# A two-layer hybrid decoder: smaller first FFN group, GpSimd products in pieces, and four reorderings at the seams

## The chip, the cores and the metric

The kernel runs on one core of a Trainium2 chip. The metric is device time in microseconds (us) of one execution; the times below are of whole executions, and the trace is of one more execution under the hardware profiler. The core has TensorE (PE), which multiplies matrices and transposes, VectorE (DVE), ScalarE (ACT) and GpSimd (POOL), and SyncE (SP), whose queue issues all transfers.

## The reference

A token stream `x` of 1024 tokens by 1024 features goes through two layers and a last norm. All of it is float32.

```python
for i in range(DEPTH):                       # 2
    proj = rms_norm(h, attn_norm[i]) @ w_in[i]
    # six latent (MLA) heads, five sparse (DSA) heads with a top-256 of an indexer's
    # scores, five stick-breaking heads, for blocks of 128 queries
    mix = heads(proj)
    h = h + mix @ w_o[i]
    hf = rms_norm(h, ffn_norm[i])
    h = h + (silu(hf @ w_gate[i]) * (hf @ w_up[i])) @ w_down[i]     # 2816 wide
    g = sigmoid(rms_norm(h, ple_norm[i]) @ w_ple_gate[i])
    h = h + g * (p[i] @ w_ple_proj[i])
return rms_norm(h, final_norm)
```

A stick-breaking head weighs key j of query t by sigmoid(z_j) times the product of sigmoid(-z) over the keys between j and t.

## The kernel before, in words

Activations lie with features on the 128 partitions and 512 tokens (a "half") in the free dimension; there are two halves and eight feature tiles of the stream, `h[0]` to `h[7]`. Every product in float32 is done as three matmuls on rounded parts (lines 266, 267, 268): weight and activation are each split into a high part and the rest, and high x high, high x rest and rest x high are summed in one PSUM tile. Of the weights (`load_cols`), ScalarE makes the high part `wh` (line 187) and GpSimd the rest `wl`, in pieces of 256 columns (line 196). Of the activations, ScalarE makes the high part and VectorE the rest.

Work is woven from two streams. The dense stream (`first`, then `layer_rest` for each layer and half) runs the output projection `w_o`, the FFN, the gated embedding (PLE) and the next layer's input projection. The attention stream (`attention`) of the next half in order runs between its matmuls. The order on TensorE is the program's own order; on the other engines and in SyncE's queue a planner with a model of times sets it when the kernel is built. Under the last half's dense part (`layer_rest(1, 1)`) no attention is left to run.

- **FFN.** 22 feature tiles (`FT`), taken in groups of four: 4, 4, 4, 4, 4, 2. For each tile, a gate and an up projection (48 matmuls) and a chain of VectorE, ScalarE and GpSimd operations (lines 624 to 641; GpSimd's is line 627) make the tile's two parts. The down projection of a group (`down`) runs behind the first tile of the next group; the last group's runs on its own behind the last tile. It goes over eight output tiles m, and for each adds its PSUM tile to `h[m]` (line 590); the last one also hands `h[m]` to the next norm (`Norm.tile`): the scaled parts (lines 314, 315), a square (325), and a sum of squares `acc` (326). PSUM has three such D tiles.
- **Norm.** `rstd` turns `acc` into row sums by TensorE (line 344) and then works out the inverse root in 12 small VectorE operations (347 to 355). `after(n, f)` runs `f` n steps later; a step is three matmuls of a dense product.
- **Stick-breaking.** For two blocks of queries at a time, ScalarE makes `P` and `A` of up to 1024 keys, VectorE runs a scan over `A` (905), GpSimd multiplies `P` by it in one instruction (908), and TensorE transposes `P` in 128 x 128 pieces (845), 256 keys at a time: `piece(0)` needs columns 0 to 255 of both.
- **The start** of `layer_rest(1, 1)` loads eight tiles of `mix` (549): four into the attention's tiles `PT`, four into the three `tmp` tiles which the dense stream also uses. ScalarE and VectorE split them (292, 293).
- **The output.** For half 0 the row sums and eight `piece`s (four transposes, a scaling and a store each) follow as hooks in the next dense part. For half 1 they end the kernel: row sums, then eight pieces one after the other, each reading all four `h` of its column.
- **The beginning.** `load_x(0)` queues half of x, the norm gains, the first weights, the other half of x. `to_features` transposes x (1206).

Of the kernel before, what the change touches and what calls it, by code (L numbers as in the profile page):

```python
# [88 lines left out]
def trunk(ctx: ExitStack, tc, x, p, w_in, attn_norm, mla_q_norm, mla_w_uq, mla_kv_norm, mla_w_ukv,  # L89
# [35 lines left out]
    def spare_tile(m):  # L125

        if m < 6:
            return ap.tile([128, T], F32, name="P" if m < 4 else "A", bufs=4 if m < 4 else 2)[:, :HALF]
        if m == 6:
            return ap.tile([128, T], F32, name="kraw")[:, :HALF]  # L130
        return ap.tile([128, NT, 64], F32, name="vraw").rearrange("p t c -> p (t c)")
# [45 lines left out]

    def split_w(raw, hi, lo, *order):
# [32 lines left out]
    def load_x(half):  # L211
        xt = []
        for c in range(2):
# [6 lines left out]
            if half == 0 and c == 0:  # L220
                load_gains()
                first_w.append(load_cols([w_in[0, :, a:b] for a, b in FIRST], DT))
# [75 lines left out]
    class Norm:  # L298
# [8 lines left out]
        def tile(self, src):  # L307
# [14 lines left out]
            else:  # L322
                with priority(AHEAD if late else 0):
                    sq = tmp_tile()
                    ACT.activation(sq, src, AF.Square)
                    (DVE if late or alone[0] else POOL).tensor_tensor(self.acc, self.acc, sq, op=ALU.add)  # L326
# [208 lines left out]
    def layer_rest(L, half):  # L535
        k = (L, half)
        mix = {}
        final = L == DEPTH - 1 and half == 1
        for i, j in enumerate(MIX_ORDER):
            if i >= 4:  # L540
                a = tmp_tile()
# [16 lines left out]
        def add(m, ps):  # L558
            hm = spare_tile(m) if final else h_tile()
# [48 lines left out]
        for g0 in range(0, FT, FG):  # L608
            fs = range(g0, min(g0 + FG, FT))
            act = []  # L610
            if fs[-1] == FT - 1:
                pr = wp.tile([128, 4, PLE], F32, name="wr", bufs=WR)
                nc.sync.dma_start(pr, p[L, 0, half * HALF:(half + 1) * HALF].rearrange("(t p) c -> p t c", p=128))
            for f in fs:
                if f == FT - 1:
                    for j in range(2):
                        after(2 + 8 * j, lambda j=j: embedding(pr, j))
# [4 lines left out]
                def gate(pg=pg, G=G, t=t):  # L622
                    with priority(EVAC):
# [3 lines left out]
                        POOL.tensor_tensor(t, t, ffn.rep, op=ALU.mult)  # L627
# [72 lines left out]
        def piece(t, c, tile):  # L700
            ps = tile()
            for d in range(4):
                PE.transpose(ps[:, d * 128:(d + 1) * 128], h[c * 4 + d][:, t * 128:(t + 1) * 128], identF)  # L703
            o = act_tile(F32)
            if c:
# [4 lines left out]
            nc.sync.dma_start(out[0, tt * 128:(tt + 1) * 128, c * HALF:(c + 1) * HALF], o)  # L710

        if half == 0:
            after(4, norm.rstd)
            for i in range(8):
                after(12 + 2 * i, lambda i=i: piece(i % 4, i // 4, T_tile))
            return
        norm.rstd()
# [600 lines left out]
```

## Time and profile before

| | |
|---|---|
| time, median of three runs (lowest, highest) | 3173.28 us (3171.9, 3175.07) |
| profiled execution, its time | 3165.42 us |
| profiled execution, its span | 3163.4 us |
| mean granted clock of TensorE over the span | 0.988 |
| busy share of the span: DVE, ACT, POOL | 67%, 47%, 54% |

The time of an execution holds a little more than the span from the first to the last instruction; here 2.0 us. The profiled execution is 7.9 us below the median of the runs.

### The profile page before, as it was taken

The page shows a single profiled execution, that of the slowest core. Times are in us where ns is not written, and L with a number is a line of the kernel's source. Part 1 is how long each engine was busy: PE and PEld are TensorE (multiplying, and loading weights), DVE is VectorE, ACT ScalarE, POOL GpSimd, SP SyncE. Part 2 cuts the span into 40 slices and gives each one's busy share as a digit, 9 for nine tenths or more (in the row PEclk, how much of TensorE's full clock was granted, in tenths as well). Part 3 has the DMA queues.
Part 4 walks back from the last instruction along what each step waited for, and adds up shares of the span by engine and source line. Part 5 has one row for each costly group of instructions (what it writes and reads, how often), then busy time and mean ns, then how long its engine had stood idle before and what let it go on. Part 6 is the DMA issues. An engine that isn't in the chain of part 4 may idle for free. (4 is left out here: it accounts for less than half of the span.)

```text
span 3163.4 us, 43510 instructions
## 1 busy us (share of the span) xinstructions
PE 3053.9 (97%) x15059; PEld 2552.8 (81%) x15059; DVE 2107.8 (67%) x3716; ACT 1484.1 (47%) x2485; POOL 1722.8 (54%) x1965
## 2 busy tenths in 40 slices
PE   8999999999999999999999999989999999999998
PEld 6777878777887888888888888777888887888876
DVE  4879756799997645687744636899996565322234
ACT  4555654445455545444444535545444455322233
POOL 4543366666445433776555744666445445666663
PEclk9999999999999999999999999999999999999998
DMA  7475553333333446433332466323323223333332
GB/s 205 119 200 143 158 166 91 96 90 88 97 103 96 108 116 178 138 104 109 109 107 85 122 162 183 114 66 102 97 90 111 83 75 124 109 97 97 99 95 67
DMA packets 549948, 363.59 MB, mean 115 GB/s; under 512 B 134671, under 2 KB 491743, under 8 KB 549727
## 3 DMA queue, kind: packets, MB, share of 16 engines
q1 hardware_dynamic: 549727, 360.81, 39.3%
q8 instruction: 119, 1.95, 0.3%
q14 instruction: 102, 0.84, 0.1%
HBM read 310.65 MB, written 50.08 MB: 114 GB/s over the span
## 5 line engine op out<-in xcount | busy, mean ns | idle before, releaser
L196 POOL TENSOR_TENSOR wl<-wr,wh 128x256 fp32r<-128x256 f32 x1684 | 1395.6, 860 | 1147.5 <-ACT wh L187 1111.5
L266 PE MATMUL D<-act,wh 128*128 128x512 f32 x3416 | 1361.0, 398 | 10.5 <-ACT act L640 2.5
L267 PE MATMUL D<-act,wh 128*128 128x512 f32 x3416 | 1342.3, 393 | 5.7 <-DVE act L315 3.4
L268 PE MATMUL D<-act,wl 128*128 128x512 f32 x3416 | 1342.0, 393 | 3.5 <-POOL wl L196 3.3
L268 PEld LDWEIGHTS D<-act,wl 128*128 128x128 f32 x3416 | 645.4, 189 | 148.0 <-POOL wl L196 6.6
L187 ACT CAST wh<-wr 128x1024 fp32r<-128x1024 f32 (+3 forms) x432 | 443.7, 1027 | 678.9 <-PE D L267 551.5
L266 PEld LDWEIGHTS D<-act,wh 128*128 128x128 f32 x3416 | 647.3, 189 | 137.8 <-ACT act L640 3.5
L267 PEld LDWEIGHTS D<-act,wh 128*128 128x128 f32 x3416 | 646.7, 189 | 134.2 <-DVE act L315 5.1
L1099 DVE TENSOR_SCALAR_CACHE_REDUCE junk<-isc,cand 128x512 uint8<-128x512 f32 (+5 forms) x396 | 371.6, 938 | 5.8
L853 DVE TENSOR_TENSOR PT<-T,PT 128x384 fp32r<-128x384 f32 (+1 forms) x320 | 201.8, 631 | 94.9 <-ACT PT L852 94.2
L852 ACT CAST PT<-T 128x384 fp32r<-128x384 f32 (+1 forms) x320 | 173.4, 542 | 120.4 <-PE T L845 115.8
L862 PEld LDWEIGHTS O<-PT,V 128*128 128x128 f32 x1280 | 195.4, 190 | 33.4 <-DVE mix L871 9.3
L805 PE MATMUL S<-kh,qh 128*128 128x384 f32 (+4 forms) x544 | 206.7, 381 | 10.8 <-ACT P L891 5.6
L845 PE MATMUL T<-identF,P 128*128 128x128 f32 x1152 | 182.5, 275 | 32.8 <-POOL P L908 30.9
L862 PE MATMUL O<-PT,V 128*128 128x256 f32 x1280 | 205.9, 284 | 6.0 <-DVE mix L871 6.0
L805 PE MATMUL S<-kl,qh 128*128 128x384 f32 (+4 forms) x544 | 203.5, 375 | 2.5 <-DVE kl L293 2.5
L908 POOL TENSOR_TENSOR P<-P,A 128x127 f32<-128x127 f32 (+3 forms) x80 | 103.2, 1294 | 163.8 <-DVE A L905 103.3
L845 PEld LDWEIGHTS T<-identF,P 128*128 128x128 f32 x1152 | 135.0, 141 | 37.6 <-POOL P L908 34.5
L1065 DVE SCALAR_TENSOR_TENSOR isc<-P,iw,isc 128x384 f32<-128x384 f32 (+2 forms) x84 | 96.0, 1143 | 85.4 <-ACT P L1059 85.1
L627 POOL TENSOR_TENSOR tmp<-tmp,rr 128x512 f32<-128x512 f32 x88 | 119.6, 1359 | 39.4 <-DVE tmp L626 35.6
L891 ACT ACTIVATE P<-S,nm 128x128 f32<-128x128 f32 (+3 forms) x116 | 79.6, 687 | 125.1 <-DVE nm L884 124.6
L624 DVE TENSOR_TENSOR tmp<-D,rr 128x512 f32<-128x512 f32 x88 | 60.5, 688 | 102.1 <-PE D L268 97.6
(213 smaller groups left out, 3263.1 us busy)
## 6 DMA issues: line engine op xcount, KB each, us to landing
wr<-in_w_gate_dram SPq DMA_DIRECT2D x88, 512.0 KB, 3.8
wr<-in_w_up_dram SPq DMA_DIRECT2D x88, 512.0 KB, 3.9
wr<-in_w_down_dram SPq DMA_DIRECT2D x80, 512.0 KB, 3.4
wr<-in_w_in_dram SPq DMA_DIRECT2D x44, 512.0 KB, 3.9
wr<-in_w_in_dram SPq DMA_DIRECT2D x76, 256.0 KB, 3.5
wr<-in_w_o_dram SPq DMA_DIRECT2D x32, 512.0 KB, 4.0
wr<-in_w_ple_gate_dram SPq DMA_DIRECT2D x32, 512.0 KB, 3.7
h<-h SPq DMA_DIRECT2D x56, 256.0 KB, 4.4
```

The source lines that it names most:

```text
L187: ACT.copy(hi, raw)
L196: POOL.tensor_tensor(l[:, ks], a[:, ks], f32(h[:, ks]), op=ALU.subtract)
L266: PE.matmul(ps, a, ah, start=first and i == 0, stop=False)
L267: PE.matmul(ps, a, al, start=False, stop=False)
L268: PE.matmul(ps, b, ah, start=False, stop=last and i == len(ks) - 1)
L627: POOL.tensor_tensor(t, t, ffn.rep, op=ALU.mult)
L805: PE.matmul(o, a, b, start=j == 0, stop=j == len(mms) - 1)
L845: PE.transpose(ps[:, o:o + 128], self.P[q][:, j * 128:(j + 1) * 128], identF)
L852: ACT.copy(pt[:, 0, o:], self.ps[:, o:])
L853: DVE.tensor_sub(pt[:, 1, o:], self.ps[:, o:], f32(pt[:, 0, o:]))
L862: PE.matmul(self.O[:, :256], self.head.V[:, j, :], pt[:, s, o:o + 256], start=j == 0 and s == 0, stop=j == 2 * self.n - 1 and s == 1)
L1099: DVE.tensor_scalar(junk[:, :n], isc[:, off[t]:off[t] + n], c[:, i:i + 1], None, op0=op, op1=ALU.add, accum_out=cnt[:, i:i + 1])
```

## The change

The FFN's first group has two feature tiles and the others four: 2, 4, 4, 4, 4, 4; the load of `p` stays at feature tile 20. In the last dense part all eight spare tiles are taken at once, and the last four `mix` loads go into the second halves of attention's four `P` tiles. In `load_x(0)` all of x is queued ahead of the first weights. GpSimd's products of lines 326, 627 and 908 are issued in pieces of 256 columns. For half 0, the hook of the row sums moves from 4 to 10 steps, and the eight pieces from 12.. to 18... For half 1, 25 of the 32 transposes of the output stand ahead of the row sums, seven behind them, and then come the eight scalings, in turn on VectorE and ScalarE.

```diff
--- before.py
+++ after.py
@@ -122,13 +122,12 @@
     def h_tile():
         return dp.tile([128, HALF], F32, name="h", bufs=8)
 
-    def spare_tile(m):
-
-        if m < 6:
-            return ap.tile([128, T], F32, name="P" if m < 4 else "A", bufs=4 if m < 4 else 2)[:, :HALF]
-        if m == 6:
-            return ap.tile([128, T], F32, name="kraw")[:, :HALF]
-        return ap.tile([128, NT, 64], F32, name="vraw").rearrange("p t c -> p (t c)")
+    def spare_tiles():
+
+        P = [ap.tile([128, T], F32, name="P", bufs=4) for _ in range(4)]
+        A = [ap.tile([128, T], F32, name="A", bufs=AS) for _ in range(2)]
+        return ([t[:, :HALF] for t in P + A] + [ap.tile([128, T], F32, name="kraw")[:, :HALF],
+                 ap.tile([128, NT, 64], F32, name="vraw").rearrange("p t c -> p (t c)")], [t[:, HALF:] for t in P])
 
     def tmp_tile(dt=F32):
         return dp.tile([128, HALF], dt, name="tmp", bufs=TMPS)
@@ -175,6 +174,13 @@
 
 
 
+    def in_pieces(out, a, b, op):
+
+        n = out.shape[1]
+        for i in range(0, n, PIECE):
+            c = slice(i, min(i + PIECE, n))
+            POOL.tensor_tensor(out[:, c], a[:, c], b[:, c], op=op)
+
     def split_w(raw, hi, lo, *order):
 
         if order:
@@ -219,7 +225,8 @@
                 xt[c].append(a)
             if half == 0 and c == 0:
                 load_gains()
-                first_w.append(load_cols([w_in[0, :, a:b] for a, b in FIRST], DT))
+        if half == 0:
+            first_w.append(load_cols([w_in[0, :, a:b] for a, b in FIRST], DT))
         return xt
 
     gains = {}
@@ -323,7 +330,10 @@
                 with priority(AHEAD if late else 0):
                     sq = tmp_tile()
                     ACT.activation(sq, src, AF.Square)
-                    (DVE if late or alone[0] else POOL).tensor_tensor(self.acc, self.acc, sq, op=ALU.add)
+                    if late or alone[0]:
+                        DVE.tensor_tensor(self.acc, self.acc, sq, op=ALU.add)
+                    else:
+                        in_pieces(self.acc, self.acc, sq, ALU.add)
 
         def tokens(self, xt):
 
@@ -536,9 +546,11 @@
         k = (L, half)
         mix = {}
         final = L == DEPTH - 1 and half == 1
+        if final:
+            spare, more = spare_tiles()
         for i, j in enumerate(MIX_ORDER):
             if i >= 4:
-                a = tmp_tile()
+                a = more[i - 4] if final else tmp_tile()
             elif final:
                 if i % 2 == 0:
                     pair = ap.tile([128, 2, HALF], F32, name="PT", bufs=PTS)
@@ -556,7 +568,7 @@
             return load_cols([w_o[L, :, m * 128:(m + 1) * 128]], DT)
 
         def add(m, ps):
-            hm = spare_tile(m) if final else h_tile()
+            hm = spare[m] if final else h_tile()
             nc.sync.dma_start(hm, h_d[half][m])
             with priority(EVAC):
                 DVE.tensor_add(hm, hm, ps)
@@ -605,13 +617,13 @@
                 yield from gemm(ps, w, act, range(len(fs)), m0=(m % 2) * 128)
                 add(m, ps)
 
-        for g0 in range(0, FT, FG):
-            fs = range(g0, min(g0 + FG, FT))
+        for end in range(FT % FG or FG, FT + 1, FG):
+            fs = range(max(end - FG, 0), end)
             act = []
-            if fs[-1] == FT - 1:
-                pr = wp.tile([128, 4, PLE], F32, name="wr", bufs=WR)
-                nc.sync.dma_start(pr, p[L, 0, half * HALF:(half + 1) * HALF].rearrange("(t p) c -> p t c", p=128))
             for f in fs:
+                if f == FT - 2:
+                    pr = wp.tile([128, 4, PLE], F32, name="wr", bufs=WR)
+                    nc.sync.dma_start(pr, p[L, 0, half * HALF:(half + 1) * HALF].rearrange("(t p) c -> p t c", p=128))
                 if f == FT - 1:
                     for j in range(2):
                         after(2 + 8 * j, lambda j=j: embedding(pr, j))
@@ -624,7 +636,7 @@
                         DVE.tensor_mul(G, pg, ffn.rep)
                         ACT.activation(t, G, AF.Tanh, scale=0.5)
                         DVE.scalar_tensor_tensor(t, t, 1.0, G, op0=ALU.add, op1=ALU.mult)
-                        POOL.tensor_tensor(t, t, ffn.rep, op=ALU.mult)
+                        in_pieces(t, t, ffn.rep, ALU.mult)
                 pu = D_tile()
                 wu = load_cols([w_up[L, :, f * 128:(f + 1) * 128]], DT)
                 if f == 0:
@@ -697,28 +709,42 @@
             yield from in_projection(L + 1, half, norm, h)
             return
 
-        def piece(t, c, tile):
-            ps = tile()
-            for d in range(4):
-                PE.transpose(ps[:, d * 128:(d + 1) * 128], h[c * 4 + d][:, t * 128:(t + 1) * 128], identF)
-            o = act_tile(F32)
-            if c:
+        def turned(ps, i, ds):
+
+            for d in ds:
+                PE.transpose(ps[:, d * 128:(d + 1) * 128], h[i // 4 * 4 + d][:, i % 4 * 128:(i % 4 + 1) * 128], identF)
+
+        def put(ps, i):
+            o, t = act_tile(F32), i % 4
+            if i >= 4:
                 ACT.activation(o, ps, AF.Copy, scale=norm.r[:, t:t + 1])
             else:
                 DVE.tensor_scalar(o, ps, norm.r[:, t:t + 1], None, op0=ALU.mult)
             tt = half * 4 + t
-            nc.sync.dma_start(out[0, tt * 128:(tt + 1) * 128, c * HALF:(c + 1) * HALF], o)
+            nc.sync.dma_start(out[0, tt * 128:(tt + 1) * 128, i // 4 * HALF:(i // 4 + 1) * HALF], o)
+
+        def piece(i):
+            ps = T_tile()
+            turned(ps, i, range(4))
+            put(ps, i)
 
         if half == 0:
-            after(4, norm.rstd)
+            after(10, norm.rstd)
             for i in range(8):
-                after(12 + 2 * i, lambda i=i: piece(i % 4, i // 4, T_tile))
+                after(18 + 2 * i, lambda i=i: piece(i))
             return
+
+        S = S_tile()
+        banks = [S[:, 0], S[:, 1], psO.tile([128, HALF], F32, name="O"), T_tile(), D_tile(), D_tile(), D_tile()]
+        for i in range(7):
+            turned(banks[i], i, range(4 if i < 4 else 3))
         norm.rstd()
-        S = S_tile()
-        tiles = [S[:, 0], S[:, 1], T_tile(), T_tile(), psO.tile([128, HALF], F32, name="O"), D_tile(), D_tile(), D_tile()]
-        for i in range(8):
-            piece(i % 4, i // 4, lambda: tiles[i])
+        for i in range(4, 7):
+            turned(banks[i], i, (3,))
+        banks.append(T_tile())
+        turned(banks[7], 7, range(4))
+        for i in (0, 4, 1, 5, 2, 6, 3, 7):
+            put(banks[i], i)
 
 
     def attention(L, half):
@@ -905,7 +931,7 @@
                 DVE.tensor_tensor_scan(A[:, :n][:, ::-1], A[:, :n][:, ::-1],
                                        zeros[:, 0:1].to_broadcast([128, n]),
                                        initial=1.0, op0=ALU.mult, op1=ALU.add)
-                POOL.tensor_tensor(P[:, :n - 1], P[:, :n - 1], A[:, 1:n], op=ALU.mult)
+                in_pieces(P[:, :n - 1], P[:, :n - 1], A[:, 1:n], ALU.mult)
                 self.P.append(P)
 
         mixes, rows = {}, {}
```

## Rows read from the trace of the kernel before

**Rows 1.** The page of the profile, its first part: busy time, share of the span and instructions of each engine.

```profile
PE 3053.9 (97%) x15059; PEld 2552.8 (81%) x15059; DVE 2107.8 (67%) x3716; ACT 1484.1 (47%) x2485; POOL 1722.8 (54%) x1965
```

**Rows 2.** The view of waits of TensorE (PE) over the whole span: the waiting line and whom it waited for, then us in total, how often, the longest in us.

```profile
PE T L845 <- POOL P L908: 30.9, 12, 3.9
PE T L344 <- DVE rr L326: 9.6, 6, 3.1
...
PE D L1206 <- DMA act<-in_x_dram: 7.0, 6, 3.5
...
PE D L267 <- DVE act L315: 3.4, 3, 1.5
```

**Rows 3.** The view of windows: for each stretch of the span its length, the busy time and instructions of each engine, the granted clock of TensorE (1.00 is 2.4 GHz, 0.50 is 1.2 GHz) and the DMA share. Four stretches that each follow a wait of TensorE.

```profile
632.80:636.20 3.40, 3.40 (x10) 2.66 (x9) 3.36 (x7) 0.81 (x1) 2.51 (x4) 0.50 0.63 187
...
2216.50:2220.00 3.50, 3.24 (x9) 2.68 (x10) 3.50 (x7) 1.10 (x2) 3.50 (x6) 0.51 0.17 58
2670.50:2677.30 6.80, 5.97 (x13) 4.42 (x14) 3.55 (x11) 2.47 (x4) 0.00 (x0) 0.50 0.34 119
3090.40:3097.20 6.80, 6.80 (x21) 5.32 (x20) 3.48 (x15) 0.00 (x0) 0.00 (x0) 0.50 0.21 63
```

**Rows 4.** The view of lines by form for GpSimd (POOL), whole span: line, engine, operation, tiles and shapes, count | busy us, mean ns of one | idle us before them and who ended it.

```profile
L196 POOL TENSOR_TENSOR wl<-wr,wh 128x256 fp32r<-128x256 f32 x1668 | 1384.3, 861 | 1138.4 <-ACT wh L187 1102.4 <-PE T L845 15.1 <-DMA qraw<-dq 5.4
...
L908 POOL TENSOR_TENSOR P<-P,A 128x1023 f32<-128x1023 f32 x10 | 21.6, 2158 | 16.3 <-DVE A L905 5.9 <-DVE inc L1113 5.8 <-PE D L268 4.6
...
L908 POOL TENSOR_TENSOR P<-P,A 128x767 f32<-128x767 f32 x10 | 15.4, 1544 | 14.0 <-DVE A L905 9.0 <-DVE rstd L355 2.7 <-DVE cand L1114 2.4
...
L908 POOL TENSOR_TENSOR P<-P,A 128x127 f32<-128x127 f32 x10 | 4.1, 412 | 13.4 <-DVE inc L1113 6.2 <-DVE A L905 4.4 <-DVE rstd L355 2.4
```

**Rows 5.** The timeline (start us, length us, engine, line, operation, tiles and shapes, count [idle before it <- releaser]) of GpSimd, VectorE (DVE) and TensorE at three places: a stick-breaking product at 629 us, a weight split at 1757 us, another at 2087 us.

```profile
629.39 2.00 POOL L908 TENSOR_TENSOR P<-P,A 128x1023 f32<-128x1023 f32 x1
629.41 2.00 DVE L1113 TENSOR_SCALAR inc<-cnt 128x4 int32<-128x4 f32 x1
631.45 0.55 PE L845 MATMUL T<-identF,P 128*128 128x128 f32 x3 [3.69 <-POOL P L908]
637.33 0.60 PE L845 MATMUL T<-identF,P 128*128 128x128 f32 x4
...
1757.11 4.16 POOL L196 TENSOR_TENSOR wl<-wr,wh 128x256 fp32r<-128x256 f32 x4
1758.34 0.50 PE L268 MATMUL D<-act,wl 128*128 128x512 f32 x1 [0.81 <-POOL wl L196]
...
2087.47 5.83 POOL L196 TENSOR_TENSOR wl<-wr,wh 128x256 fp32r<-128x256 f32 x4 [1.62 <-ACT wh L187]
```

**Rows 6.** The timeline of TensorE at the start of the last down projection of layer 0, half 0.

```profile
969.44 0.40 PE L267 MATMUL D<-act,wh 128*128 128x512 f32 x1
969.68 0.40 PE L268 MATMUL D<-act,wl 128*128 128x512 f32 x1
972.53 0.50 PE L266 MATMUL D<-act,wh 128*128 128x512 f32 x1 [2.46 <-ACT act L640]
974.22 0.79 PE L267 MATMUL D<-act,wh 128*128 128x512 f32 x1 [1.18 <-DVE act L641]
974.81 0.63 PE L268 MATMUL D<-act,wl 128*128 128x512 f32 x1
975.23 0.63 PE L266 MATMUL D<-act,wh 128*128 128x512 f32 x1
```

**Rows 7.** The timeline of SyncE's queue (SPq) and TensorE at the start of the last output projection.

```profile
2666.59 1.00 SPq L549 DMA_DIRECT2D tmp<-mix  x2
...
2667.91 1.02 PE L344 MATMUL T<-ones,rr 128*128 128x1 f32 x8 [2.11 <-DVE rr L326]
2671.33 0.80 PE L266 MATMUL D<-act,wh 128*128 128x512 f32 x1 [2.39 <-ACT act L292]
```

**Rows 8.** The timeline of SyncE's queue, ScalarE (ACT) and TensorE at the start of the kernel.

```profile
6.74 2.00 SPq L218 DMA_DIRECT2D act<-in_x_dram  x4
...
11.36 1.04 ACT L187 CAST wh<-wr 128x1024 fp32r<-128x1024 f32 x1 [0.40 <-DMA wr<-in_w_in_dram]
...
12.09 1.05 PE L1206 MATMUL D<-identF,act 128*128 128x128 f32 x2 [1.76 <-DMA act<-in_x_dram]
...
13.47 3.64 PE L1206 MATMUL D<-identF,act 128*128 128x128 f32 x14 [0.33 <-DMA act<-in_x_dram]
...
16.77 0.78 PE L266 MATMUL D<-act,wh 128*128 128x512 f32 x1
```

**Rows 9.** The timeline of all engines at the end of the kernel.

```profile
3148.18 1.66 PE L344 MATMUL T<-ones,rr 128*128 128x1 f32 x8 [3.06 <-DVE rr L326]
...
3152.33 0.75 DVE L708 TENSOR_SCALAR act<-S,rstd 128x512 f32<-128x512 f32 x1
3153.11 7.07 SPq L710 DMA_DIRECT2D out_dram<-act  x8
3153.13 1.12 PE L703 MATMUL S<-identF,P 128*128 128x128 f32 x4 [2.34 <-DVE act L708]
...
3158.55 1.27 ACT L706 ACTIVATE act<-D,rstd 128x512 f32<-128x512 f32 x2 [0.17 <-PE D L703]
...
3158.68 0.27 PE L703 MATMUL D<-identF,kraw 128*128 128x128 f32 x1
```

## The prediction

> **What bounds the kernel now.** I read the engines' shares first: TensorE is busy for 97% of the span [rows 1], so only two things can shorten it, less work on TensorE or fewer of its waits. The change removes no matmul. I therefore went to the waits of TensorE [rows 2], then to the timeline around each, then to the granted clock behind it. The reader should see three things. The largest wait is not for weights but for the stick-breaking product on GpSimd: 30.9 us in 12 waits. The next ones belong to seams: row sums that wait for a norm's sum of squares (9.6 us), the first transposes that wait for x (7.0 us), a projection that waits for a norm's scaled parts (3.4 us). And a wait is paid twice: behind many of those of 2 us and more stands a stretch at the lower clock [rows 3], in which matmuls start 0.42 us apart (974.81 to 975.23) where they stood 0.24 us apart before it (969.44 to 969.68) [rows 6]. At those spacings a stretch at 1.2 GHz loses 43% of its length: 1.5 us of one of 3.4 us, 2.9 us of one of 6.8 us.
>
> **GpSimd's products in pieces.** Of the waiting product, TensorE needs columns 0 to 255 first. In rows 5 the product of 1023 columns runs from 629.39 for 2.00 us, and three transposes start at 631.45 after a wait of 3.69 us. That a reader may start on the first piece is shown at 1757: GpSimd works on four weight pieces from 1757.11 for 4.16 us, and the matmul that needs the first starts at 1758.34 [rows 5]. One piece costs, on the line through 127 columns (412 ns) and 767 (1544 ns), 1.77 ns per column and 0.64 us for 256; the weight pieces of that size take 0.86 us on average [rows 4]. Waiting products have 767 or 1023 columns, so a wait shrinks by 1544 - 861 = 0.68 us at least and 2158 - 640 = 1.52 us at most: 8 to 18 us over 12 waits. I take 14, nearer the upper end, since the one in rows 5 is a 1023. Below that the bound is nothing, should the earlier links (a late scan, weights ahead in GpSimd's queue) move by as much; above it the whole 30.9 us. Shorter waits also leave fewer stretches at the lower clock. Behind these waits I count six, the first at 632.8 and the last at 2216.5 [rows 3], one of them (2093.7) 6.8 us long, the others 3.4: 5 x 1.5 + 2.9 = 10.4 us lost, of which I take 6. Sum: -20 us (bounds 0 and -41).
> The extra cost, four pieces for 4 x 0.64 = 2.56 us where one took 2.00, falls on later columns; their transposes come at 637.33, 5.9 us behind the first [rows 5], which hides it. The pieces of lines 326 and 627 lengthen work that hides under a projection of 24 matmuls, 24 x 0.24 = 5.8 us; I cost them at nothing, and at 0.4 us for each of the 88 gate chains if the cover fails.
> There is a second effect. A VectorE operation on 128 x 4 elements (line 1113) starts at 629.41 and lasts 2.00 us, as long as the GpSimd product beside it [rows 5]: something holds it until the product ends. With pieces it would be held 0.64 us. I book nothing for it. The Trainium skill (SBUF - State Buffer, Who interferes with whom) says why: the two share a pair of ports, taken for a whole instruction, and the second to issue blocks fully. By that rule the change also gives VectorE gaps in which to step in, which is the rival below.
>
> **Groups of 2, 4, 4..** No matmul is added; what changes is the cover of the last down projection. With two tiles, 2 x 3 matmuls stand ahead of the first use of the last tile's parts; these came late by 2.46 us (high part, 972.53) and again by 1.18 us (rest, 974.22), and then ran at the lower clock [rows 6]. With four, 6 x 3 matmuls (4.3 us) stand there, 2.9 us more. And the norm's work per output tile gets 12 matmuls (2.9 us) instead of six (1.4 us). At these four seams: 3.6 us [rows 6] + 1.5 us for its stretch at 1.2 GHz + the 3.4 us for scaled parts (line 315) [rows 2] + 2.9 us for the stretch at 3090.4 [rows 3] + about 2 us of the row sums' 9.6: of these, 2.1 us stand at the last mix [rows 7] and 3.1 at the end [rows 9], and of the remaining 4.4 I take half. Sum -13.4 us; I take -13 (bounds -5 and -18). Against it, the group of two now stands first, woven with attention: its evacuations come every 1.4 us while VectorE also serves the heads. I add +4 us (0 to +9). The load of `p` stays where it was and costs nothing.
>
> **The last mix.** Two waits stand here: 2.11 us for the sum of squares (the moved hook gives it 6 x 3 matmuls, 4.3 us, more) and 2.39 us for a split whose load was queued only at 2666.59, when a `tmp` tile came free [rows 7]. Behind them 6.8 us run at 1.2 GHz [rows 3]. All gone: 2.1 + 2.4 + 2.9 = 7.4 us. Splits that come earlier press on VectorE, so I take -6.5 (bounds -2 and -8: if only the hook helps, the split is still late). The eight pieces move with the hook under later `w_o` matmuls; their stores pass in SyncE's queue among weight loads and cost nothing there, as the queue has two further weight buffers to run ahead.
>
> **The end.** Before, TensorE sits idle 3.06 us ahead of the row sums; second transposes wait 2.34 us for the first scaling; scalings go on from 3152.33 to 3158.55 + 1.27 = 3159.8, because transposes run between them [rows 9]. After, 25 transposes fill the idle time: four took 0.60 us [rows 5], so 2.8 us from 3145.1, or 3.8 at the worst, against row sums at 3148.2. Then eight scalings of 0.75 and 0.64 us run two at a time, 3.1 us instead of 7.5. That would give 4.4 us; but eight stores of 256 KB, issued over 7.07 us before [rows 9], have to land in a shorter time, so I take -2.5 (bounds 0 and -5).
> The Trainium skill (TensorE: Matmul & The Clock Gate, PE-mode transpose) says that transposes do not engage the full clock; by that rule the 25 would be done late, row sums would start some 2 us later, and the end would give nothing. Here four took 1.12 us at 3153.13, and with nothing but transposes in between one took 0.27 us at 3158.68 [rows 9], as at 637.33, where four took 0.60 us [rows 5]: the full clock came, which speaks against the rule.
>
> **The beginning.** The second half of x is queued at 6.74 us, behind the weights; transposes wait 1.76 us for it and end near 17.1, and the first product starts at 16.77. Weights arrive for ScalarE at 11.36 [rows 8]. After, x comes earlier by the two weight loads and the weights later by four x loads; the product could start when both are there, at about 14.5. I take -2 us (bounds +1.5 and -2.5).
>
> **Sum.** -20 - 13 + 4 - 6.5 - 2.5 - 2 = -40 us. Against the profiled execution's 3165.4 us this is 3125.4; the runs' median lies 7.9 us above it, so 3133.3, predicted 3133 us, 1.3% less. A change of 0.2% (6.3 us) is about what can be told from none.
>
> **The rivals.**
> - *Likeliest, 0.60:* as summed, 3133 us, own range 3120 to 3148.
> - *The pieces bring nothing, 0.20.* The wait's start is a scan on a full VectorE or weights ahead of the product, and the planner puts other pieces in front. For it: in the stretch at 2087 four weight pieces take 5.83 us [rows 5] just before a product. Against: even then the first piece still ends earlier than the whole. Time: 3133 + 20 = 3153 us.
> - *VectorE steps between the pieces, slower, 0.05.* Place: the products of 640 and more columns, 40 of them. If four pieces stretch as the weight pieces at 2087 did, to 5.83 us, the last ones end about when the next transposes come, 5.9 us on [rows 5]. The other parts give 20 us, so this ends slower by more than 0.2% once each of the 40 costs TensorE (20 + 6.3) / 40 = 0.66 us. At 1 us: 3173.3 + 40 - 20 = 3193 us. Against it: only the columns from 256 on are concerned, and each step needs 256 more.
> - *The new order costs elsewhere, 0.08.* The planner reorders four engines for the new program; other waits grow by as much as the seams give. 3133 + 36 = 3169, about no change.
> - *More than forecast, 0.07.* Nearly all of the product waits and their slow stretches go, and VectorE, no longer held, is ahead: 3133 - 21 = 3112 us.
>
> **How the numbers follow.** Faster: the first and last case, nearly all of the second, a quarter of the fourth, 0.88; same: half of the fourth and the edge of the second, 0.05; slower: the third and the last quarter of the fourth, 0.07. The range holds 8 in 10 if it leaves out the third and part of the fourth and last: 3112 to 3160 us.
>
> **What would show it.** In the changed kernel's waits, the wait of transposes for the product should fall from 30.9 to 15 us or less, and a product's four pieces should overlap the first transposes. The last down projections should show no wait for line 640, and the stretches at 974.1, 2670.5 and 3090.4 should have no counterpart at 1.2 GHz. The start of the last output projection should run through. At the end, transposes should stand ahead of the row sums and the last scaling should come some 3 us behind the inverse root. I am wrong if the product wait stays near 30 us, if evacuations of the first group stall TensorE by more than 9 us, or if new stretches at 1.2 GHz appear in the heads' part.

## The result, and the profile after

The changed kernel takes 3136.8 us (median of four runs, 3134.5 to 3138.7); the kernel before, run beside it, 3172.6 us (3167.7 to 3175.1). The ratio is 0.9897 with a 95% interval of 0.9885 to 0.9909: 1.0% faster, 33 us by the ratio. Forecast were 3133 us. The profiled execution of after takes 3137.5 us, its span 3135.8 us.

The page of after, its first part, against [rows 1]:

```profile
PE 3042.1 (97%) x15059; PEld 2543.7 (81%) x15059; DVE 2091.9 (67%) x3716; ACT 1487.1 (47%) x2485; POOL 1779.6 (57%) x2218
```

The same number of matmuls and of VectorE instructions; GpSimd has 253 more, the pieces. TensorE is still busy for 97%.

The waits of TensorE in after, over the whole span (waiting line and whom it waited for; us in total, times, longest), against [rows 2]. Line 182 is the helper that issues GpSimd's products in pieces, 871 the transposes, 354 the row sums, 334 the sum of squares on VectorE:

```profile
PE T L871 <- POOL P L182: 23.1, 11, 4.6
...
PE T L354 <- DVE rr L334: 4.1, 5, 2.9
```

The product wait fell from 30.9 us to 23.1, not to the 15 or less of the forecast. The wait for the sum of squares fell from 9.6 to 4.1 us. The wait for the norm's scaled parts (3.4 us before) is not in the view any more, and neither is one for an evacuation of the down projection. Over all lines of the view, TensorE's waits fell from 104 us to 82.

Where in the span the time was won, read from the starts of the same row sums in both traces:

| stretch that ends at row sums | before, us | after, us | won |
|---|---|---|---|
| start to those of the first FFN | 133.6 | 134.2 | -0.6 |
| on to the end of FFN (0,0) | 1001.4 | 990.9 | 11.1 |
| on to the end of FFN (0,1) | 1765.0 | 1754.6 | -0.1 |
| on to the end of FFN (1,0) | 2597.6 | 2586.4 | 0.8 |
| on to the FFN norm of (1,1), with the last mix | 2724.5 | 2708.6 | 4.7 |
| on to the last FFN's norm | 3092.2 | 3070.1 | 6.2 |
| on to the final row sums | 3148.2 | 3123.7 | 2.4 |
| on to the end of the span | 3163.4 | 3135.8 | 3.1 |

The two executions are 27.6 us apart, less than the medians, since the profiled execution of before was a short one; the table is read for places. The gain stands in FFN (0,0), which is woven with heads of the first layer, and behind 2597. FFN (1,0), which has the same weave and four of the 11 product waits (2084 to 2205), won almost nothing: those four sum to 10.2 us, the four there before to 11.3. Two changes work against each other there: by the traces of the experiments below, the new groups alone lengthen this stretch (the 0.8 us row) by 5.2 us, and the pieces, with the groups as in after, shorten it by 7.9 us. The stretch to the end of FFN (0,0) is shortened by both, 4.8 and 9.0 us.

**A product in pieces.** The timelines of GpSimd, VectorE and TensorE at two of the 11 waits (start, length, engine, line, operation, count [idle before it]); each fence is one engine. First GpSimd, at 670 and 2083 us:

```profile
664.88 5.04 POOL L202 TENSOR_TENSOR wl<-wr,wh 128x256 fp32r<-128x256 f32 x4 [2.47 <-issue]
669.88 2.87 POOL L182 TENSOR_TENSOR P<-P,A 128x256 f32<-128x256 f32 x4
...
2075.56 4.46 POOL L182 TENSOR_TENSOR tmp<-tmp,rr 128x256 f32<-128x256 f32 x2
2079.98 3.24 POOL L202 TENSOR_TENSOR wl<-wr,wh 128x256 fp32r<-128x256 f32 x4
2083.18 2.96 POOL L182 TENSOR_TENSOR P<-P,A 128x256 f32<-128x256 f32 x4
```

The scans on VectorE ahead of these products, and of the one at 2033:

```profile
664.61 2.28 DVE L931 TENSOR_TENSOR_SCAN A<-A,zeros 128x1024 f32<-128x1024 f32 x1
...
2030.63 2.31 DVE L931 TENSOR_TENSOR_SCAN A<-A,zeros 128x1024 f32<-128x1024 f32 x1
...
2076.67 2.81 DVE L931 TENSOR_TENSOR_SCAN A<-A,zeros 128x1024 f32<-128x1024 f32 x1
```

And TensorE's transposes:

```profile
670.57 0.90 PE L871 MATMUL T<-identF,P 128*128 128x128 f32 x3 [4.56 <-POOL P L182]
...
2034.08 0.69 PE L871 MATMUL T<-identF,P 128*128 128x128 f32 x2 [3.99 <-POOL P L182]
...
2084.40 0.90 PE L871 MATMUL T<-identF,P 128*128 128x128 f32 x3 [3.73 <-POOL P L182]
```

At 669.88 the pieces begin, at 670.57 the transposes: 0.69 us, where 2.06 us lay between them at 629.39 in [rows 5]. That step holds. But the scan ends at 664.61 + 2.28 = 666.89, and the first piece starts 2.99 us later, behind four weight pieces that took 5.04 us. At 2083 it is 3.70 us, behind two pieces of a gate product and four of weights. At 2034 the scan itself is late: TensorE is free from 2030.09, and the scan ends at 2032.94. Cutting every wait into three, the scan's end against the moment when TensorE came free, the queue from the scan to the product, and the product until the transposes start, gives, with the two experiments that make pairs of the same groups:

| us, sum over the waits | before (12) | pieces alone (12) | after without pieces (13) | after (11) |
|---|---|---|---|---|
| scan ends later (or, negative, earlier) than TensorE is free | -3.9 | 3.2 | -2.6 | 1.8 |
| from the scan's end to the product's start | 9.9 | 13.4 | 12.0 | 12.9 |
| from the product's start to the transposes | 24.9 | 9.1 | 25.4 | 8.4 |
| wait | 30.9 | 25.7 | 34.8 | 23.1 |

From before to after the product's own part fell by 16.5 us; 8.7 of them came back ahead of it, 5.7 through scans that came late against TensorE and 3.0 in GpSimd's queue. But these two kernels also differ in the groups, which move the heads. In the old order the pieces take 15.8 us off the product's part and 10.6 come back; in the new order they take off 17.0 and 5.3 come back, so there the wait falls by 11.7 us.

A full VectorE is a likely reason for the late scans; no run tests it alone. The windows of this weave in FFN (0,0) (length, then busy time and instructions of PE, PEld, DVE, ACT, POOL; clock; DMA), and behind them those of the same weave in layer 1. Before:

```profile
600.00:800.00 200.00, 182.59 (x920) 150.26 (x919) 198.23 (x306) 97.17 (x144) 128.56 (x123) 0.98 0.30 89
2010.00:2220.00 210.00, 185.10 (x907) 152.12 (x906) 202.27 (x326) 104.09 (x153) 132.69 (x127) 0.94 0.30 87
```

After:

```profile
600.00:800.00 200.00, 186.81 (x951) 153.73 (x949) 198.09 (x318) 99.85 (x150) 146.22 (x185) 0.99 0.32 94
2000.00:2210.00 210.00, 188.51 (x931) 155.78 (x930) 201.92 (x326) 105.00 (x156) 147.65 (x188) 0.94 0.30 88
```

VectorE is busy for 99% of the stretch in FFN (0,0) in both kernels, while its share of the span is 67%; TensorE is at 91 to 93% here. Busy holds time in which VectorE is held by GpSimd, as the 2.00 us of line 1113 in [rows 5], whose median in that trace is 0.17 us. In this stretch VectorE does 318 instructions where it did 306, with the same busy time, and 3% more matmuls run beside them. In layer 1 it is busy for 96% and does 326 instructions before and after, while the matmuls also grow by 3%, 931 for 907.

**The seams.** The one seam that kept its waits is the first, at the end of FFN (0,0): a matmul of its last down projection waits for the rest part of the last tile (line 653, 641 before), then the row sums wait, and the window behind them runs at half clock (1.2 GHz).

```profile
952.91 0.50 PE L274 MATMUL D<-act,wh 128*128 128x512 f32 x1 [1.87 <-DVE act L653]
...
990.91 1.75 PE L354 MATMUL T<-ones,rr 128*128 128x1 f32 x8 [2.85 <-DVE rr L334]
```

```profile
990.90:997.70 6.80, 6.79 (x25) 6.22 (x26) 2.75 (x14) 0.90 (x2) 0.00 (x0) 0.51 0.44 113
```

Before, this seam had waits of 2.46, 1.18 and 1.68 us, 5.3 in all, and 3.4 us at 1.2 GHz at 974.1; now it has 4.7 us and, with 3.4 us at 953.5, 10.2 us at 1.2 GHz. So the stretch up to here was not won at the seam.

At the last mix next to nothing of [rows 7] is left (0.2 us for the row sums): 35 us there with TensorE busy for 33.0, at full clock.

```profile
2645.00:2680.00 35.00, 33.01 (x159) 26.07 (x158) 27.02 (x42) 19.41 (x31) 23.79 (x26) 1.00 0.44 134
```

**The end**, against [rows 9]: TensorE, then VectorE, then ScalarE, then SyncE's queue.

```profile
3120.21 0.39 PE L275 MATMUL D<-act,stg 128*128 128x512 f32 x1
3120.44 1.03 PE L715 MATMUL S<-identF,P 128*128 128x128 f32 x8
3121.31 0.60 PE L715 MATMUL O<-identF,P 128*128 128x128 f32 x4
...
3123.06 0.27 PE L715 MATMUL D<-identF,kraw 128*128 128x128 f32 x1
3123.66 1.02 PE L354 MATMUL T<-ones,rr 128*128 128x1 f32 x8 [0.34 <-DVE rr L334]
```

```profile
3127.10 1.41 DVE L722 TENSOR_SCALAR act<-S,rstd 128x512 f32<-128x512 f32 x2
...
3129.09 0.74 DVE L722 TENSOR_SCALAR act<-T,rstd 128x512 f32<-128x512 f32 x1
```

```profile
3127.16 1.84 ACT L720 ACTIVATE act<-D,rstd 128x512 f32<-128x512 f32 x3 [3.62 <-DVE rstd L365]
...
```

```profile
3127.87 4.49 SPq L724 DMA_DIRECT2D out_dram<-act  x8
```

The 25 transposes take 2.9 us from 3120.44, in the gap; eight scalings take 2.7 us from 3127.10 to 3129.83; the stores are issued over 4.49 us instead of 7.07. The transposes also run faster: the granted clock is 1.00 from 3120.4 to 3123.4, where before the row sums and 30 of the 32 transposes stood in a stretch at 1.2 GHz, shown here with the one behind it. They start 0.11 us apart instead of 0.21.

```profile
3148.40:3158.60 10.20, 7.86 (x38) 7.46 (x38) 4.97 (x16) 1.42 (x3) 0.00 (x0) 0.50 0.29 111
3158.60:3162.00 3.40, 0.46 (x4) 0.22 (x2) 0.00 (x0) 1.22 (x2) 0.00 (x0) 1.00 0.75 287
```

**The beginning**, against [rows 8]: SyncE's queue, then TensorE.

```profile
5.56 2.02 SPq L224 DMA_DIRECT2D act<-in_x_dram  x4
7.62 1.06 SPq L211 DMA_DIRECT2D wr<-in_w_in_dram  x2
```

```profile
11.85 1.77 PE L1232 MATMUL D<-identF,act 128*128 128x128 f32 x13 [0.32 <-DMA act<-in_x_dram]
15.44 0.50 PE L273 MATMUL D<-act,wh 128*128 128x512 f32 x1 [1.82 <-ACT wh L193]
```

The first product starts 1.3 us earlier, now after a wait for the weights; by the row sums at 134 us nothing of it is left.

### The profile page after: what moved, and what is told of

It reads as the page before. It is cut to its first block, busy times and chain, and to the rows that moved or that the text cites. A ratio compares the mean times of both kernels' runs of the same rounds, so it can differ in the third digit from the quotient of the medians.

```text
span 3135.8 us, 43786 instructions
## 1 busy us (share of the span) xinstructions
PE 3042.1 (97%) x15059; PEld 2543.7 (81%) x15059; DVE 2091.9 (67%) x3716; ACT 1487.1 (47%) x2485; POOL 1779.6 (57%) x2218
## 4 chain that ended last, share of the span: by engine, by line
PE 71%; DVE 19%; DMA 4%; issue 2%; POOL 2%; ACT 1%; SPq 0%; DVEq 0%; ACTq 0%; POOLq 0%
PE D L273 19%; PE D L275 19%; PE D L274 19%; PE S L831 6%; DVE junk L1125 6%; PE O L888 3%; PE T L871 3%; DVE A L931 2%; DVE PT L879 2%; POOL wl L202 1%; DVE nm L910 1%; DVE h L602 1%; DVE act L322 1%; DVE cand L1140 1%; PE T L354 1%
## 5 line engine op out<-in xcount | busy, mean ns | idle before, releaser
L275 PEld LDWEIGHTS D<-act,wl 128*128 128x128 f32 x3416 | 644.5, 189 | 151.8 <-POOL wl L202 11.1
L871 PE MATMUL T<-identF,P 128*128 128x128 f32 x1152 | 182.1, 275 | 23.1 <-POOL P L182 23.1
L182 POOL TENSOR_TENSOR P<-P,A 128x256 f32<-128x256 f32 (+1 forms) x200 | 126.6, 659 | 124.6 <-DVE A L931 76.9
L182 POOL TENSOR_TENSOR tmp<-tmp,rr 128x256 f32<-128x256 f32 x176 | 144.2, 839 | 30.8 <-DVE tmp L638 27.7
```

The costliest lines, as they stand in the source:

```text
L182: POOL.tensor_tensor(out[:, c], a[:, c], b[:, c], op=op)
L275: PE.matmul(ps, b, ah, start=False, stop=last and i == len(ks) - 1)
L871: PE.transpose(ps[:, o:o + 128], self.P[q][:, j * 128:(j + 1) * 128], identF)
```

## The experiments

Ratios are to the kernel before, run beside it, with 95% intervals; "us" of a ratio is its distance from 1 times 3172.6. An interval is about 4 us wide on either side.

**Pieces alone** (the kernel before, and of the diff the three places of `in_pieces` only).

```diff
-                POOL.tensor_tensor(P[:, :n - 1], P[:, :n - 1], A[:, 1:n], op=ALU.mult)
+                in_pieces(P[:, :n - 1], P[:, :n - 1], A[:, 1:n], ALU.mult)
...
```

> The kernel before with GpSimd's three products in pieces and nothing else. The prediction's sum: -20 us (about 3153 us), the wait of transposes for the product at 15 us or less. The two traces, read side by side: the wait fell from 30.9 to 23.1 us, so about -9 us (3163). The rival that the pieces bring nothing: within 3 us of before, the product's wait still near 30 us.

Measured: 0.9971 (0.9961 to 0.9981), 9 us. Product wait 25.7 us in 12 waits; the wait for the sums of squares rises to 12.9. Less than half of the forecast's 20. The trace is of the slowest of nine executions.

**Groups alone** (the kernel before, with the FFN's groups of 2, 4, 4..).

```diff
-        for g0 in range(0, FT, FG):
-            fs = range(g0, min(g0 + FG, FT))
+        for end in range(FT % FG or FG, FT + 1, FG):
+            fs = range(max(end - FG, 0), end)
...
```

> The kernel before with FFN groups of 2, 4, 4, 4, 4, 4 and nothing else. The prediction's sum: -9 us (-13 for the seams, +4 for the first small group), no wait for line 640 at the last down projections. If the gain of the whole comes from the pieces, this one gives less than 4 us. If the first small group stalls on its evacuations, slower than before.

Measured: 0.9956 (0.9944 to 0.9969), 14 us, although the heads are met in another phase and the product wait rises. Two rows of its waits, for the product and for an evacuation:

```profile
PE T L845 <- POOL P L908: 34.8, 13, 5.8
...
PE D L266 <- DVE h L590: 0.7, 1, 0.7
```

The first small group does not stall TensorE; before, the waits for `h` of the same line were 2.0 us, at 738.63 and 753.19, in the middle of FFN (0,0). Against before, this trace wins 6.0 us on the way to the last FFN's norm and loses 5.2 us in the stretch to the end of FFN (1,0).

**After without pieces** (all three places whole again).

```diff
-                in_pieces(P[:, :n - 1], P[:, :n - 1], A[:, 1:n], ALU.mult)
+                POOL.tensor_tensor(P[:, :n - 1], P[:, :n - 1], A[:, 1:n], op=ALU.mult)
...
```

> The changed kernel with GpSimd's three products whole again. The prediction's sum: +20 us on the changed kernel, about 3157 us. By the two traces: +9 us, 3146. By the rival that the pieces bring nothing: 3137, and the product's wait as in the changed kernel.

Measured: 0.9942 (0.9930 to 0.9955), 14 us slower than after. So pieces are worth 9 us in the old order and 14 in the new, though the intervals allow the two to be alike. Its product wait:

```profile
PE T L871 <- POOL P L934: 34.8, 13, 5.7
```

This is the cleanest pair for the pieces. The product wait differs by 11.7 us; all other waits of TensorE sum to 58 us here and 59 in after.

**After without groups** (4, 4, .. 2 again).

```diff
-        for end in range(FT % FG or FG, FT + 1, FG):
-            fs = range(max(end - FG, 0), end)
+        for g0 in range(0, FT, FG):
+            fs = range(g0, min(g0 + FG, FT))
```

> The changed kernel with groups of 4, 4, 4, 4, 4, 2 again. The prediction's sum: +9 us on the changed kernel, 3146 us, with waits for lines 640 and 641 back at the last down projections. If groups and other parts overlap in what they save, less than that.

Measured: 0.9951 (0.9939 to 0.9963), 17 us slower than after. Waits that come back or grow (in after the first is 4.1 us and the last 1.9, the other two are gone):

```profile
PE T L354 <- DVE rr L334: 6.7, 6, 2.2
...
PE D L274 <- DVE act L322: 3.6, 4, 1.5
...
PE D L273 <- ACT act L652: 2.4, 1, 2.4
...
PE D L274 <- DVE act L653: 2.3, 4, 1.2
```

**Only the stick product in pieces** (after, with the sums of squares and the gate products whole).

```diff
-                        in_pieces(self.acc, self.acc, sq, ALU.add)
+                        POOL.tensor_tensor(self.acc, self.acc, sq, op=ALU.add)
...
-                        in_pieces(t, t, ffn.rep, ALU.mult)
+                        POOL.tensor_tensor(t, t, ffn.rep, op=ALU.mult)
```

> The changed kernel with pieces for the stick-breaking product alone; the sums of squares and the gates' product are whole again. If the gain comes from the early first piece of the stick-breaking product: as the changed kernel, 3137 us within 3. If pieces help because they free VectorE, which the gates' product holds too: 5 us or more slower. In the changed kernel's trace two pieces of the gates' product take 4.46 us around a scan of 2.81 us just ahead of a stick-breaking product; if that is what keeps the wait at 23 us, this one is up to 5 us faster.

Measured: 0.9898 (0.9883 to 0.9914), as after. The other two places are worth nothing that can be measured, although VectorE's busy time over the span, by the page, is 2101.7 us here and 2091.9 in after, for the same 3716 instructions.

**First piece and rest** (as the one before, with the product in two: 256 columns, then all others in one).

```diff
-                in_pieces(P[:, :n - 1], P[:, :n - 1], A[:, 1:n], ALU.mult)
+                for c in (slice(0, min(PIECE, n - 1)), slice(PIECE, n - 1)):
+                    if c.start < n - 1:
+                        POOL.tensor_tensor(P[:, c], P[:, c], A[:, c.start + 1:c.stop + 1], op=ALU.mult)
```

> As product_pieces, but the stick-breaking product in two: columns 0 to 255, then all the rest. If only the first piece matters to TensorE: the same time as product_pieces within 3 us. If the gain comes from VectorE being held for shorter times: the rest of 767 columns holds it 1.5 us, and the time is 5 us or more above product_pieces.

Measured: 0.9917 (0.9904 to 0.9931), 6 us slower than the stick product in four pieces; the intervals overlap, so this is likely and not certain. It is slower although its product wait is the lowest of all (23.4 us with four pieces):

```profile
PE T L871 <- POOL P L936: 19.2, 10, 4.5
PE O L888 <- DVE mix L897: 8.8, 7, 2.4
```

The wait for `mix` grew; with four pieces it is

```profile
PE O L888 <- DVE mix L897: 5.5, 5, 2.0
```

VectorE's busy time is 2107.9 us here and 2101.7 with four pieces. But TensorE's waits in all are no longer, 80 us here and 82 there; it is TensorE's busy time that is longer, 3050.0 us and 3044.9. What makes this version slower stays open.

**Stick chain first** (after, with both sigmoids, the scan and the product under the planner's priority EVAC).

```diff
+                with priority(EVAC):
...
```

> The changed kernel with the stick-breaking chain (two sigmoids, scan, product) planned ahead of other work, as evacuations are. If what is left of the product's wait (23.1 us) is the queue in front of it (weight pieces and gate pieces on GpSimd, counting operations on VectorE): the wait falls below 12 us and the time to some 3125 us. If the planner's order is not what sets it: as the changed kernel. If the chain now delays weights or the gates: slower.

Measured: 0.9892 (0.9879 to 0.9906), no difference from after; the wait is 23.2 us in 11. The priority hardly changed the order at the waits, so this tells nothing of what an earlier scan would bring.

**First piece on VectorE** (after, in the second halves' heads: columns 0 to 255 by VectorE behind the scan, the rest by GpSimd).

```diff
-                in_pieces(P[:, :n - 1], P[:, :n - 1], A[:, 1:n], ALU.mult)
+                if half:
+                    DVE.tensor_tensor(P[:, :PIECE], P[:, :PIECE], A[:, 1:PIECE + 1], op=ALU.mult)
+                    in_pieces(P[:, PIECE:n - 1], P[:, PIECE:n - 1], A[:, PIECE + 1:n], ALU.mult)
...
```

> The changed kernel, but in the heads of the second half the first 256 columns of the stick-breaking product are made by VectorE right behind its scan; GpSimd makes the others. In the changed kernel's trace the first piece starts 0.1 to 3.7 us behind the scan's end at the eleven places where TensorE waits. If GpSimd's queue (and what holds it) is what keeps the wait at 23.1 us: the wait falls to about 9 us and the time by 10 us or more, to 3125. If the late scan is what sets it: the wait falls by less than 5 us, and the 40 more VectorE operations leave the time the same or make it slower.

Measured: 0.9950 (0.9936 to 0.9963), 17 us slower than after, where I had expected a gain. Its waits:

```profile
PE T L871 <- DVE P L935: 30.8, 10, 6.8
...
PE T L871 <- DVE inc L1143: 5.2, 1, 5.2
```

VectorE's timeline at the second of these lines, a wait that ends at 675.24 and that the view puts down to the small operation behind the piece:

```profile
668.40 2.82 DVE L931 TENSOR_TENSOR_SCAN A<-A,zeros 128x1024 f32<-128x1024 f32 x1
671.15 1.25 DVE L1129 TENSOR_SCALAR_CACHE_REDUCE junk<-isc,cand 128x1024 uint8<-128x1024 f32 x1
...
672.33 0.68 DVE L636 TENSOR_TENSOR tmp<-D,rr 128x512 f32<-128x512 f32 x1
673.04 1.14 DVE L803 TENSOR_TENSOR qh<-qraw,qh 64x512 fp32r<-64x512 f32 x1
674.21 0.56 DVE L879 TENSOR_TENSOR PT<-T,PT 128x384 fp32r<-128x384 f32 x1
674.68 0.41 DVE L935 TENSOR_TENSOR P<-P,A 128x256 f32<-128x256 f32 x1
```

Between the scan's end (671.2) and the piece (674.68) VectorE does four other things. And the 40 instructions take 22.6 us, on an engine that is busy for 99% there; its busy time over the span rises from 2091.9 to 2109.2 us. Both fit the loss; which of the two weighs more this run does not tell.

**Last mix without the spare tiles** (after; loads 4 to 7 of the mix in `tmp` tiles again, the hook kept).

```diff
-                a = more[i - 4] if final else tmp_tile()
+                a = tmp_tile()
```

> The changed kernel with the last four mix loads in the tmp tiles again, the later hook kept. The prediction's sum gives loads and hook together 6.5 us and says the hook alone is worth 2: 4.5 us slower than the changed kernel, 3141 us, with a wait for line 293's or 292's split back. If the hook does it all: 3137.

Measured: 0.9919 (0.9906 to 0.9933), 7 us slower than after; the intervals just overlap. The wait is back, longer than in [rows 7]:

```profile
2658.45 0.79 PE L273 MATMUL D<-act,wh 128*128 128x512 f32 x1 [6.26 <-ACT act L299]
```

Around it 10.2 us run at 1.2 GHz:

```profile
2654.20:2664.40 10.20, 5.95 (x13) 4.42 (x14) 2.74 (x4) 2.48 (x4) 0.76 (x2) 0.50 0.55 181
```

**Hook as before** (after; the norm's root behind four operations, the pieces behind 12).

```diff
-            after(10, norm.rstd)
+            after(4, norm.rstd)
...
-                after(18 + 2 * i, lambda i=i: piece(i))
+                after(12 + 2 * i, lambda i=i: piece(i))
```

> The changed kernel with the hook of half 0's row sums at 4 steps and its pieces from 12 again. The prediction: the wait for the sum of squares at the last output projection (2.1 us before) is back, and with it some of the stretch at 1.2 GHz: 2 to 4 us slower than the changed kernel, 3140. If the sum of squares is in time anyway: 3137.

Measured: 0.9911 (0.9898 to 0.9924), 4 us slower, within the intervals; the wait it was meant for is back in the trace:

```profile
2662.60 1.02 PE L354 MATMUL T<-ones,rr 128*128 128x1 f32 x8 [2.63 <-DVE rr L334]
```

**Old end** (after; row sums first, then each piece's transposes and scaling).

```diff
-        for i in range(7):
-            turned(banks[i], i, range(4 if i < 4 else 3))
         norm.rstd()
...
+        for i in range(8):
+            turned(tiles[i], i, range(4))
+            put(tiles[i], i)
```

> The changed kernel with the end in its old order: row sums first, then the eight pieces one after the other. The prediction's sum: 2.5 us slower (0 to 5), 3139; by the trace from the row sums' start to the end of the span: 12.1 us in the changed kernel, 15.2 us here as before. If transposes alone ran at 1.2 GHz, the end would be the same.

Measured: 0.9910 (0.9897 to 0.9924), 4 us slower, within the intervals. In the trace, row sums to end take 14.9 us (3122.1 to 3137.0) against 12.1 in after.

**Weights between the halves of x** (after, with the load order of before).

```diff
-        if half == 0:
-            first_w.append(load_cols([w_in[0, :, a:b] for a, b in FIRST], DT))
+                first_w.append(load_cols([w_in[0, :, a:b] for a, b in FIRST], DT))
```

> The changed kernel with the first weights queued between the halves of x again. The prediction's sum: 2 us slower, 3139. By the trace the first product starts at 15.44 us in the changed kernel and should start near 16.8 here; if the beginning's gain is lost again within the next hundred us, as the row sums at 134 us in both traces hint (133.6 before, 134.2 after), the time is the same within 2 us.

Measured: 0.9899 (0.9883 to 0.9915): no difference. The first product starts at 16.02 us, 0.6 later than in after and 0.75 earlier than before, so not all of the 1.3 us was the load order's.

## Why the prediction was right, and where its steps were not

The direction, the 1% and the place inside the range (3112 to 3160) are right; 3133 against 3136.8 us. That it came so near is in part luck, as terms that were too large and too small cancel. Taken out of after one at a time they come to 14 (pieces), 17 (groups), 7 + 4 (mix and hook), 4 (end), 0 (beginning): 46 us against 33 for the whole. Each of these differences carries after's own interval, so the excess may be noise; a part whose gain hangs on another one counts twice in such a sum, as mix and hook do.

- **Pieces, -20: mis-sized; 9 alone, 14 in company.** The early start on the first piece is shown, and the product's own part fell by 16.5 us (15.8 and 17.0 in the pairs with the same groups) where I took 14. What failed is the step from there to TensorE's wait and to 6 us of clock gained. The wait fell by 7.8 us, by 5.2 in the old order and 11.7 in the new, as 5.3 to 10.6 us came back ahead of the product; stretches at 1.2 GHz behind product waits sum to 20.4 us in after and 23.9 before, which at the prediction's 43% is 1.5 us and not 6. I had priced that as a rival (scan on a full VectorE, weights ahead of the product), all or nothing; the truth lies between it and the forecast. The reading that I left out is VectorE's share in this stretch: 99%, where I went on from the 67% of [rows 1]. That a shorter product only lets TensorE arrive earlier at a scan which a full VectorE holds back fits the table; it is not tested apart.
- **VectorE held by GpSimd, booked at nothing: seen, its worth not shown.** For the same 3716 instructions VectorE's busy time over the span is 2112.8 us without pieces, 2107.9 with first piece and rest, 2101.7 with the product in pieces and 2091.9 with all three. That this brings time is argued from the slower version in two pieces and from the 12 more instructions at 600 to 800 us. Against it stand the last 9.8 us, which brought none, the weave of layer 1, where VectorE does no more instructions, and the pair with the new groups, in which TensorE's other waits do not fall: there the product's own wait, 11.7 us, is most of the 14. The Trainium skill (SBUF - State Buffer, Who interferes with whom) says that a VectorE operation with two inputs from SBUF contends with a GpSimd instruction that reads SBUF, over a shared pair of ports which is an exclusive lock; this trace agrees, with two gate pieces that took 4.46 us around a scan of 2.81 us.
- **The rival of VectorE between the pieces** (slower) did not come: four pieces took 2.87 us at 669.88, 2.96 us at 2083.18, and at most 3.63 us in the ten products of 1023 columns, not 5.83.
- **Groups, -13 + 4: too small; 14 alone, 17 in company.** The waits that I added up went, but for those of the first seam: 5.3 us became 4.7, and 3.4 us at 1.2 GHz became 10.2, so the stretch at 974.1 has a counterpart against the forecast. The +4 for the first small group was wrong as a wait for evacuations: none shows in after. What the new order does cost, 5.2 us up to the end of FFN (1,0), likely comes with the heads that it moves.
- **Last mix, -6.5: a little large, 4.7 us by the traces.** Both waits but 0.2 us and the stretch of 6.8 us are gone. The stretch from the end of FFN (1,0) to the next norm takes 122.2 us in after and 126.9 before, 128.8 without the spare tiles and 127.4 with the old hook: by these traces each of the two brings nothing without the other, so their 7 and 4 us cannot be added, and the lower bound of -2, "if only the hook helps", was too hopeful. Without the tiles the split comes 6.26 us late instead of 2.39, likely because the place is reached sooner.
- **End, -2.5: right to a little low.** 3.1 us by the traces. Transposes fill the gap, the scalings take 2.7 us where I had 3.1. The Trainium skill (TensorE: Matmul & The Clock Gate, PE-mode transpose) says that the full clock does not engage for transposes. These traces do not agree: four took 0.60 us at 3121.31, right behind the last products, as they did in [rows 5], and before the change the granted clock rose to 2.4 GHz at 3158.6, behind 10.2 us in which TensorE ran row sums and transposes alone.
- **Beginning, -2: nothing.** The product did start earlier (by 1.3 us, forecast 2.3, and about half of it by the load order), but what follows up to 134 us does not start earlier for it; which work sets that was not tried.

Of the forecast's signs of being wrong one came in part: new stretches at 1.2 GHz in the heads' part. After has 6.8 us at 2370.0, behind a wait of 1.38 us, where before has none between 2220 and 2670.

No version was found that beats the changed kernel by more than the intervals.

## What to carry to other kernels

Read the engines' shares by stage before a wait is priced: an engine at 67% of the span was at 99% in the very stretch where the largest wait stood. Cutting a GpSimd operation so that its reader starts on the first piece took two thirds of that operation's own length out of the wait (25.4 to 8.4 us); but price the wait as a chain, for a third to two thirds of this came back as a late scan or a longer queue ahead of it. Two fixes at one place can need each other, and then neither is worth anything alone. Put the short group of a pipelined loop where other work covers it, not ahead of a seam.

## What was not expected of the hardware

- The clock after a wait is not set by that wait alone. The wait of 3.03 us that ends at 2166.75 in after has no stretch at 1.2 GHz behind it, the shorter one of 2.15 us that ends at 2126.23 has 3.4 us:

```profile
2166.70:2175.00 8.30, 8.25 (x44) 7.02 (x45) 8.23 (x17) 3.70 (x6) 8.28 (x11) 1.00 0.33 102
2126.00:2135.00 9.00, 8.77 (x39) 7.34 (x40) 8.83 (x19) 4.25 (x7) 6.62 (x10) 0.81 0.27 82
```

Stretches at 1.2 GHz sum to 64.6 us in the profiled execution of after and 78.7 in that of before, and to between 55.7 and 103.5 us in those of the experiments, though these differ by little; that of the pieces alone has the most, so its gain may be small in part for this and not for the pieces.
- Four weight pieces that stand beside a scan of 2.28 us take 5.04 us, 1.26 us each, where the mean over the span is 0.86 us; a product piece without such company takes 0.64 us, as the line through the whole products in [rows 4] had it.
